# Eight experts on one core: the store of expert 6 goes behind the last load in the GpSimd ring, the store of expert 5 goes out in halves

## The chip, the cores and the metric

The kernel runs on one NeuronCore of a Trainium2 chip. The metric is the device time of one execution in microseconds, as the median of several runs. The profile is that of one execution; its span (first to last instruction) is a little shorter than the time that is measured.

The engines that matter here are PE (matmuls), DVE and ACT (copies out of PSUM, and the ReLU on ACT), GpSimd (POOL in the profile) and SyncE (SP), which here do little but issue DMAs. GpSimd's DMAs form one queue, called the ring below and q0 in the profile; SyncE's form another, q1; ACT has q10. All run on the same 16 DMA engines.

## The reference

Eight experts, each a two-layer perceptron on its own 256 rows, all in float32:

```python
n_experts, capacity, hidden, expert_hidden = 8, 256, 512, 2048
h = np.matmul(x, w1) + b1[:, np.newaxis, :]
h = np.maximum(h, 0)
return (np.matmul(h, w2) + b2[:, np.newaxis, :]).astype(np.float32)
```

One expert has 4 MB of `w1`, 4 MB of `w2`, 0.5 MB of `x` and 0.5 MB of output. No weight is used twice by different experts, so every byte is read once.

## The kernel before

**Staging.** Matmuls are done in fp16. The weights and most of `x` are cast from float32 to fp16 by the DMA that loads them, and all of these loads are issued by GpSimd. `x` of the first two experts comes as float32 by SyncE and ACT, so that the ring can begin with `w1`.

**Per expert.** `first_product(e)` (line 112) makes h transposed, 128 of the 2048 hidden units at a time: four matmuls into one PSUM tile `ph`, then a ReLU with bias on ACT (line 119) into `hT`. In its middle it transposes `x` of the next expert (line 99). `second_product(e)` (lines 162 and 174) starts each of two accumulators `acc` (one for each half `tb` of the rows) with the bias and adds 16 matmuls of 512 columns. The output rows are dealt so that each partition holds two neighbouring rows: its stores are rows of 4 KB per partition.

**Order of the stages.** The loop at the end runs over stages `s`: the first product of expert `s`, then the second product of expert `s - LAG`, with `LAG = 3`. So the second products run three experts behind.

**Order of the DMAs.** The list `ring` is the order, written out by hand, in which GpSimd issues: per stage the loads of `x`, `w1` and `w2`, and from stage 6 on a `flush`, which is the store of an expert done earlier. The list is kept in program order. GpSimd waits at the head of its queue, so what stands behind a waiting issue waits too. By the waits in the trace, a ring transfer also waits for the landing of the eighth one before it.

**The end.** `w2` of the last expert comes in eight pieces, called pieces 1 to 8 below, in this order (rows `j` of the 16, columns):

```python
        (0, 4, 0, H), (4, 7, 0, H), (7, 10, 0, H), (10, 12, 0, H),
        (12, 14, 0, HL), (14, 16, 0, HL), (12, 14, HL, H), (14, 16, HL, H),
```

With `HL = 320`, the last expert's output has a block of 320 columns, which is finished and stored first, and one of 192. `flush(4)` stands between pieces 1 and 2; after piece 8 nothing follows in the ring.

**The stores.** `store(e, ...)` copies the two accumulators to SBUF, one by DVE (line 137), one by ACT (line 138), and then has three ways. The 192-column block of the last expert goes out by SyncE and ACT, one half of the rows each (lines 141 and 142). For `e <= RING` (0 to 4) the store is only noted in `pending`, and `flush` (line 131) issues it from GpSimd at its place in the ring. All others (5, 6 and the 320-column block of 7) are issued by SyncE as soon as the copies are done (line 148); `PARTS` could cut them into groups of partitions, and is empty. The staging tiles of experts 0 to 6 share three buffers; the last expert's have their own.

Of the kernel before, what the change touches and what calls it, by code (L numbers as in the profile page):

```python
# [11 lines left out]
def kernel(  # L12
# [17 lines left out]
    nJ = M // P  # L30
    HL = 320
    LAG = 3
    RING = 4
    PARTS = {}
    nXF32 = 2

    def ordered(ins):
# [95 lines left out]
    def store(e, po, c0, c1, split):  # L133
        w = c1 - c0
        pool = out_pool if w == H else singles
        out_sb = pool.tile([P, nTB, w], fp32, tag=f"out{c0}_{w}", name=f"out{w}")
        nc.vector.tensor_copy(out=out_sb[:, 0, :], in_=po[0])  # L137
        nc.scalar.copy(out=out_sb[:, 1, :], in_=po[1])  # L138
        dst = out[e].rearrange("(p tb) h -> p tb h", tb=nTB)[:, :, c0:c1]
        if split and c1 == H:  # L140
            nc.sync.dma_start(out=dst[:, 0, :], in_=out_sb[:, 0, :])
            nc.scalar.dma_start(out=dst[:, 1, :], in_=out_sb[:, 1, :])
        elif e <= RING:
            pending[e] = (dst, out_sb)
        else:
            step = P // PARTS.get(e, 1)
            for lo in range(0, P, step):
                nc.sync.dma_start(out=dst[lo : lo + step], in_=out_sb[lo : lo + step])

    def second_product(e):  # L150
# [18 lines left out]
        for lo, hi, p0, p1, t in w2_sb[e]:  # L169
            mine = [b for b in blocks if p0 <= b[0] and b[1] <= p1]  # L170
            for tb in range(nTB):
                for j in range(lo, hi):
                    for c0, c1, _, _ in mine:
                        ordered(nc.tensor.matmul(  # L174
                            out=acc[c0, tb],
                            lhsT=hT[e][:, j, tb * P : (tb + 1) * P],
                            rhs=t[:, j - lo, c0 - p0 : c1 - p0],
                            start=False,
                            stop=(j == nJ - 1),
                        ))  # L180
            if hi == nJ:
                for c0, c1, _, _ in mine:
                    store(e, [acc[c0, tb] for tb in range(nTB)], c0, c1, e == E - 1)
# [36 lines left out]
    ring = []  # L220
# [9 lines left out]
    e = E - LAG - 1  # L230
    for piece in (
        (0, 4, 0, H), (4, 7, 0, H), (7, 10, 0, H), (10, 12, 0, H),
        (12, 14, 0, HL), (14, 16, 0, HL), (12, 14, HL, H), (14, 16, HL, H),
    ):
        ring.append((0, load_w2_piece, (E - 1,) + piece))
        if e <= RING:
            ring.append((e + LAG + 1, flush, (e,)))
            e += 1

    for s in range(E + LAG):  # L240
        while ring and ring[0][0] <= s:
# [37 lines left out]
```

## Time and profile before

| | |
|---|---|
| time, median of 3 runs | 185.75 us (185.68 to 185.85) |
| span of the profile | 183.8 us |
| PE busy | 137.3 us, 75% |
| ACT busy | 62.7 us, 34% |
| DVE busy | 13.3 us, 7% |
| GpSimd busy | 21.0 us, 11% |
| mean DMA rate | 221 GB/s (40.58 MB) |
| read from HBM, written to HBM | 71.39 MB, 4.19 MB |
| SyncE store of expert 5 | issued at 160.9, landed 8.2 us later |
| SyncE store of expert 6 | issued at 168.5, landed 7.1 us later |
| ring stores of experts 0 to 4 | landed 48.4, 43.7, 40.1, 28.0 and 18.3 us after issue |
| SyncE store of the 320-column block | issued at 179.5, landed 2.8 us later |

The profile's DMA bytes count a cast load by what it writes, in fp16, while "read from HBM" counts the float32 that it reads; so 1 MB of loads and 1 MB of stores are different amounts of work. The share of DMA engines is the time of their packet records over 16 engines' time, and can go a little over 1 where records overlap. "To landing" is the time from a DMA's issue to its completion; for a ring transfer it includes the wait behind the transfers ahead of it. Times on the engines are those of the trace from the start of the span.

### The profile page before, as it was taken

To read this page: it belongs to the slowest core of one execution; us is meant where nothing else is said; L and a number is where in the kernel's file an instruction comes from. 1 tells how busy PE (TensorE), PEld (TensorE's weight loads), DVE (VectorE), ACT (ScalarE), POOL (GpSimd) and SP (SyncE) were. 2 spreads that over 40 slices of the span, in tenths; PEclk is the share of its full clock that TensorE was granted. 3 is DMA by queue.
4 is the path that set the end of the run, shared out by engine and by line. 5 is a ranking of instruction groups with operands and counts; after the bars stand their busy time and mean duration, and the time that the engine had idled before them with its cause. 6 is when DMAs were issued, how large, how long until landed. Compare 5 with 4: busy or idle time off the path is not lost.

```text
span 183.8 us, 2205 instructions
## 1 busy us (share of the span) xinstructions
PE 137.3 (75%) x946; PEld 98.2 (53%) x946; DVE 13.3 (7%) x22; ACT 62.7 (34%) x138; POOL 21.0 (11%) x44
## 2 busy tenths in 40 slices
PE   0555969487471999569991999529999996998581
PEld 0544959387461846556491846427469543344360
DVE  0320101001000101010100100001010010101000
ACT  0022869578260422715081513605129310101001
POOL 7100030301200011011011002000022004113000
PEclk9999999999876699979999699965999999999998
DMA  5999999899999999999999999899999999999993
GB/s 185 283 207 198 228 228 210 184 233 230 228 203 196 228 228 217 194 216 228 228 210 200 217 228 228 191 266 225 207 200 270 240 209 260 214 275 310 261 151 116
DMA packets 7017, 40.58 MB, mean 221 GB/s; under 512 B 1216, under 2 KB 2256, under 8 KB 4960
## 3 DMA queue, kind: packets, MB, share of 16 engines
q0 software_dynamic: 5584, 37.76, 95.3%
q1 hardware_dynamic: 976, 2.00, 3.1%
q10 hardware_dynamic: 448, 0.69, 1.1%
q8 instruction: 7, 0.11, 0.2%
q14 instruction: 2, 0.02, 0.0%
HBM read 71.39 MB, written 4.19 MB: 411 GB/s over the span
## 4 chain that ended last, share of the span: by engine, by line
DMA 70%; PE 14%; issue 9%; another core or an unknown queue 3%; POOL 2%; ACT 0%; POOLq 0%
DMA x<-in_x_dram 24%; DMA w2sb<-in_w_dram 21%; DMA w1sb<-in_w_dram 13%; DMA w<-in_w_dram 12%; PE ph L112 6%; PE acc L174 6%; PE psx L99 1%; POOL w2sb L84 1%; POOL w1sb L74 1%; POOL out_dram L131 0%; PE acc L162 0%; POOL b_sb L190 0%; POOL ident masks.py:199 0%; POOL ident masks.py:197 0%
## 5 line engine op out<-in xcount | busy, mean ns | idle before, releaser
L112 PE MATMUL ph<-xT,w1sb 128*128 128x256 f16 x512 | 68.2, 299 | 11.6 <-DMA w1sb<-in_w_dram 11.6
L119 ACT ACTIVATE hT<-ph,b1T 128x256 f16<-128x256 f32 x128 | 57.0, 474 | 44.2 <-PE ph L112 44.2
L112 PEld LDWEIGHTS <-w1sb 128*128 128x128 f16 x512 | 61.5, 149 | 17.7 <-DMA w1sb<-in_w_dram 12.6
L174 PE MATMUL acc<-w2sb,hT 128*128 128x512 f16 x224 | 49.5, 379 | 1.6 <-DMA w2sb<-in_w_dram 1.6
L174 PEld LDWEIGHTS <-hT 128*128 128x128 f16 x288 | 27.2, 98 | 35.0 <-issue 9.0
L138 ACT COPY out<-acc 128x512 f32<-128x512 f32 (+2 forms) x9 | 4.9, 543 | 62.0 <-PE acc L174 62.0
L99 PE MATMUL psx<-ident,x 128*128 128x128 f16 x64 | 6.7, 266 | 18.8 <-DMA x<-in_x_dram 18.1
L99 PEld LDWEIGHTS <-x 128*128 128x128 f16 x64 | 5.2, 127 | 19.8 <-DMA x<-in_x_dram 19.0
L105 DVE COPY xT<-psx 128x1024 f16<-128x1024 f16 x8 | 5.5, 692 | 82.2 <-PE psx L99 82.2
L74 POOL DMA_DIRECT2D w1sb<-in_w_dram x8 | 4.4, 554 | 59.6 <-PE ph L112 58.8
L137 DVE COPY out<-acc 128x512 f32<-128x512 f32 (+2 forms) x9 | 5.7, 632 | 75.5 <-PE acc L174 75.5
L174 PE MATMUL acc<-w,hT 128*128 128x320 f16 (+1 forms) x64 | 7.7, 272 | 3.8 <-DMA w<-in_w_dram 3.7
L84 POOL DMA_DIRECT2D w2sb<-in_w_dram x8 | 4.3, 537 | 49.4 <-PE acc L174 49.4
L205 PE MATMUL pb<-ident,b_rows 16*64 16x16 f32 x64 | 3.7, 265 | 6.8 <-DMA b_rows<-in_b_dram 6.8
L205 PEld LDWEIGHTS pb<-ident,b_rows 16*64 16x64 f32 x64 | 3.6, 198 | 6.8 <-issue 6.8
L90 POOL DMA_DIRECT2D w<-in_w_dram x8 | 5.0, 623 | 13.0 <-DMA w2sb<-in_w_dram 8.8
L119 ACT ACT_TABLE_LOAD x1 | 1.3, 1283 | 11.2 <-DVE b1T L213 11.2
L131 POOL DMA_DIRECT2D out_dram<-out x5 | 2.7, 540 | 19.5 <-ACT out L138 13.1
L162 PE MATMUL acc<-b_sb,ones 1*128 1x512 f16 (+2 forms) x18 | 4.8, 355 | 0.0
L68 POOL DMA_DIRECT2D x<-in_x_dram x6 | 3.3, 546 | 7.2 <-DMA w2sb<-in_w_dram 5.1
L162 PEld LDWEIGHTS <-ones 1*128 1x128 f16 x18 | 1.1, 92 | 2.2 <-issue 2.1
L200 DVE CAST x<-x 128x1024 f16<-128x1024 f32 x2 | 1.4, 694 | 4.5 <-DMA x<-in_x_dram 4.5
(9 smaller groups left out, 2.6 us busy)
## 6 DMA issues: line engine op xcount, KB each, us to landing
w1sb<-in_w_dram POOLq DMA_DIRECT2D x8, 2048.0 KB, 33.7
w2sb<-in_w_dram POOLq DMA_DIRECT2D x6, 2048.0 KB, 45.7
out_dram<-out POOLq DMA_DIRECT2D x5, 512.0 KB, 40.1
w2sb<-in_w_dram POOLq DMA_DIRECT2D x2, 1024.0 KB, 24.6
x<-in_x_dram POOLq DMA_DIRECT2D x6, 256.0 KB, 39.0
out_dram<-out SPq DMA_DIRECT2D x2, 512.0 KB, 7.6
w<-in_w_dram POOLq DMA_DIRECT2D x2, 384.0 KB, 20.8
x<-in_x_dram SPq DMA_DIRECT2D x1, 512.0 KB, 4.7
```

The lines of the kernel that those rows point to most:

```text
L74: ordered(nc.gpsimd.dma_start(out=w1_sb[e], in_=w1[e].rearrange("(p kc) m -> p kc m", kc=nKC)))
L84: ordered(nc.gpsimd.dma_start(out=t[:, lo : lo + step, :], in_=src[:, lo : lo + step, :]))
L90: ordered(nc.gpsimd.dma_start(out=t, in_=src[:, lo:hi, c0:c1]))
L99: ordered(nc.tensor.transpose(out=pt[:, kc, tb * P : (tb + 1) * P], in_=x16[e][:, tb, :].rearrange("p (q kc) -> p q kc", kc=nKC)[:, :, kc] ...
L105: nc.vector.tensor_copy(out=xT[e], in_=pt)
L112: ordered(nc.tensor.matmul(out=ph, lhsT=w1_sb[e][:, kc, :].rearrange("p (q j) -> p q j", j=nJ)[:, :, j], rhs=xT[e][:, kc, :], start=(kc == 0),
L119: nc.scalar.activation(out=hT[e][:, j, :], in_=ph, func=mybir.ActivationFunctionType.Relu, bias=b1T[:, j, e : e + 1], scale=1.0,)
L137: nc.vector.tensor_copy(out=out_sb[:, 0, :], in_=po[0])
L138: nc.scalar.copy(out=out_sb[:, 1, :], in_=po[1])
L162: ordered(nc.tensor.matmul(out=t, lhsT=ones1, rhs=b2_sb[0:1, e * H + c0 : e * H + c1], start=True, stop=False,))
L174: ordered(nc.tensor.matmul(out=acc[c0, tb], lhsT=hT[e][:, j, tb * P : (tb + 1) * P], rhs=t[:, j - lo, c0 - p0 : c1 - p0], start=False, sto ...
L205: ordered(nc.tensor.matmul(out=pb[s * 64 : (s + 1) * 64, j, :, :], lhsT=b1_rows.rearrange("r (q j) -> r q j", j=nJ)[:, :, j], rhs=ident[0 ...
```

## The change

The store of expert 6 (512 KB) is no longer issued by SyncE when its copies are done, but noted and issued by GpSimd behind piece 8, as the last entry of the ring. It is meant to keep the store out of the way of the last pieces of the weights. The store of expert 5, still on SyncE, is issued as two DMAs of 64 partitions (256 KB) each. The stores of experts 0 to 4 and those of the last expert keep their places.

```diff
-    RING = 4
-    PARTS = {}
+    LATE = (6,)
+    RING = (0, 1, 2, 3, 4) + LATE
+    PARTS = {5: 2}
...
-        elif e <= RING:
+        elif e in RING:
             pending[e] = (dst, out_sb)
         else:
             step = P // PARTS.get(e, 1)
...
         ring.append((0, load_w2_piece, (E - 1,) + piece))
-        if e <= RING:
+        if e in RING and e not in LATE:
             ring.append((e + LAG + 1, flush, (e,)))
             e += 1
+    for e in LATE:
+        ring.append((e + LAG + 1, flush, (e,)))
```

## The prediction

> **What bounds the kernel now.** I read the page first, then the chain of waits, then the last 25 us by timeline, windows and DMA queues.
>
> The page shows which resource never rests: the row of DMA shares, the two queues, and the chain by engine.
>
> ```profile
> DMA  5999999899999999999999999899999999999993
> ...
> q0 software_dynamic: 5584, 37.76, 95.3%
> q1 hardware_dynamic: 976, 2.00, 3.1%
> ...
> DMA 70%; PE 14%; issue 9%; another core or an unknown queue 3%; POOL 2%; ACT 0%; POOLq 0%
> ```
>
> The 16 DMA engines are at 0.9 or more from the second slice to the last but one, and the GpSimd ring (q0) alone fills 95.3% of them. PE is busy 75% and waits. So what counts is when the last bytes of the weights land, and what else the engines carry before that.
>
> The chain of waits (start, length, what) shows how the end comes about:
>
> ```profile
> 113.67 39.47 DMA w2sb<-in_w_dram
> 153.14 0.28 issue
> 153.43 21.99 DMA w<-in_w_dram
> 175.41 0.04 issue
> 175.45 3.88 PE acc L174 x32
> 179.34 0.02 issue
> 179.35 0.50 PE acc L174 x4
> 179.85 0.02 issue
> 179.88 0.32 ACT out L138
> ```
>
> The last expert's w2 comes in eight pieces. The chain runs through the third, issued at 153.43 and landed at 175.41; then PE does the rest of the product in 4.40 us. By the view of line 90, window by window, the later pieces land at 176.6 (154.68 + 21.9), 177.5 (159.48 + 18.0), 178.2 (164.41 + 13.8), 178.8 (166.13 + 12.7) and 179.34 (169.34 + 10.0). The last weight load, at 179.35, follows the landing of piece 8 at once, so PE and the DMA tail are tied. In the timeline PE has only two short idle stretches after 175.45:
>
> ```profile
> 178.30 0.89 PEld L174 LDWEIGHTS <-hT 128*128 128x128 f16 x8 [0.16 <-issue]
> ...
> 179.35 0.26 PEld L174 LDWEIGHTS <-hT 128*128 128x128 f16 x3 [0.17 <-issue]
> ```
>
> Without these PE needs 4.40 - 0.33 = 4.1 us after piece 3. If all pieces come earlier by the same time, the end moves by that time.
>
> Now the store in question. By the view of line 148, expert 6's SyncE store is issued at 168.5 and lands 7.1 us later, at 175.6, about when piece 3 lands. The DMA view of 172 to 176 shows what it takes (packets, MB, share of 16 engines):
>
> ```profile
> q0 software_dynamic: 409, 0.55, 76.9%
> q1 hardware_dynamic: 141, 0.51, 33.8%
> ```
>
> In those 4 us the ring moved 0.55 MB and SyncE's queue 0.51 MB: the whole of the store. The windows compare the stretches (after the clock: DMA share, GB/s):
>
> ```profile
> 156.00:160.00 4.00, 4.00 (x20) 1.73 (x18) 0.69 (x1) 0.00 (x0) 0.52 (x1) 1.00 1.03 215
> ...
> 172.00:176.00 4.00, 2.02 (x17) 1.55 (x17) 0.00 (x0) 0.00 (x0) 0.00 (x0) 1.00 1.11 266
> 176.00:178.00 2.00, 2.00 (x20) 1.64 (x18) 0.00 (x0) 0.00 (x0) 0.00 (x0) 1.00 1.29 172
> 178.00:180.00 2.00, 1.82 (x15) 1.09 (x13) 0.78 (x2) 0.55 (x2) 0.00 (x0) 1.00 0.27 32
> ```
>
> PE is idle for half of 172 to 176, waiting for pieces, while the engines carry the store; from 178 to 180 they are nearly empty (0.27).
>
> **What the Trainium skill says.** Three places on its page "DMA: Bandwidth & Descriptors" bear on this. Section "Queues, rings and completion order": each engine takes turns between the queues that have work, packet by packet, and within a ring descriptors are consumed in order. The trace agrees with the first: the store takes 33.8% beside the ring's 76.9%. So a store on SyncE's queue overtakes loads issued long before it, and one behind the last load in the ring does not. Section "Issuing engines are not separate DMA queues": all issuers run on the same 16 engines, so the change saves no bandwidth; it can only alter the order. The trace agrees, the shares adding up to 1.03 to 1.11. Section "Rules for kernel authors": of two transfers to disjoint partition halves it says "Don't bother — they serialize". No row of the kernel before shows halves.
>
> **The change part by part.**
>
> *Store 6 leaves SyncE's queue.* Its cost in engine time is 33.8% of 4 us = 1.35 us. Two other readings bound it. From the page, q1 took 3.1% of 183.8 = 5.7 us for 2.00 MB, so 0.524 MB cost 1.49 us. From the rates, the ring made 0.55 MB in 4 us = 138 GB/s; without the store it makes 215 with large packets (156 to 160) and 172 with the smallest (176 to 178). Taking 195, between them, it lost 57 x 4 = 0.23 MB, or 1.17 us; with 215 it lost 0.31 MB, or 1.43 us. Records overlap somewhat, the share being 1.11 in this stretch and not 1; the highest share that I can blame on the pieces alone is between 1.03 and 1.29. I take 1.35 / 1.09 = 1.24 us, and keep 0.9 and 1.5 as ends. So piece 3 lands at 175.4 - 1.2 = 174.2, piece 8 at 179.34 - 1.24 = 178.1. PE: from piece 3, 174.2 + 4.1 = 178.3; from piece 8, 178.1 + 0.5 = 178.6. The later sets it: 178.6, against 179.85.
>
> *Store 6 joins the GpSimd ring behind piece 8.* One issue of 0.54 us (the row of line 131), on an engine that has nothing behind it. It waits for three things: the issue of piece 8, ending at 170.05 (169.34 + 0.71); the ACT copy of expert 6, ending at 168.47; and, if the pattern of the waits on GpSimd holds (each ring transfer waits for the eighth before it: piece 3 for w2 of expert 5, piece 4 for the store of expert 2), the landing of store 4, at 152.0 + 18.3 = 170.3. So it is issued by about 171, seven us before its turn. Nobody waits for its landing but the end of the program. Its bytes flow as the engines run out of pieces: before, the DMA share began to fall at 177.8 and was nothing at 179.1 to 179.4; 1.24 earlier and 1.35 longer, the store is through by 179.5. That lies beside PE's last matmuls, the copies and the issue of the last stores.
>
> *The last stores.* The 320-column store was issued at 179.49 and landed 2.8 us later; it is now issued at 178.25. Its own bytes come late in those 2.8 us: the engines stood empty from 179.4 and the packet records of that queue begin at about 181.2, 1.7 us after the issue. So they begin at 179.9, 0.4 us after store 6 is through. I charge nothing; if the two meet, the bound is 0.5 us of shared engines. The stretch from the end of PE to the end of the span, 183.8 - 179.85 = 3.95 us, is kept.
>
> *Store 5 in two halves.* One more SyncE issue of 0.35 us, with nothing behind it on SyncE until 178, and the same bytes at the same place in the stream, so zero; bounds -0.2 and +0.3 us, since no row shows 64-partition stores. It had 8.2 us to landing before, and nobody waits for its buffer: it goes into the third of the three, and the only later tile of that pool, expert 6's, takes the first.
>
> *The queue tests (line 143 and the loop that fills the ring)* move nothing else: stores 0 to 4 stay between the same loads.
>
> Sum: 185.75 - 1.24 = 184.5 us, a span near 182.6.
>
> **The rivals.** *Partial gain.* The slowest engine is the one that counts, and it may gain less than the mean, or the last stores meet store 6 and give 0.5 us back. For it: the fall of the share from 177.8 to 179.1 shows that engines do not end together. Against it: a store of 128 equal rows loads all engines alike. Gain 0.4 to 0.9, some 0.65: 185.1.
>
> *No change.* The store used time that the loads could not, or the tail eats the gain whole. For it: the share of 1.11 against 1.03, and 266 GB/s moved against 215. Against it: a loaded byte is counted as fp16 but read as fp32, so bytes of loads and stores are not alike, and the ring's own rate fell to 138. 185.7.
>
> *Slower.* The last stores are treated as store 6 was: amid the ring's traffic a SyncE store took 7.1 to 8.2 us to land, after it 2.8. If the ring still holds store 6 when the 320-column store is issued, it may lose part of the difference of 4.3; with half of it, 2.15, the time is 185.75 - 1.24 + 2.15 = 186.7. Against it: only 1.3 us of the ring is left at that moment, not a stream of many us.
>
> **How the numbers follow.** Full gain (0.9 to 1.5) 0.62 at 184.5; partial 0.18 at 185.1; none 0.11 at 185.7; slower 0.09 at 186.7. A gain of over 0.2% is one of over 0.37 us, so faster 0.80, same 0.11, slower 0.09. The low end is the upper bound of the store's cost with the halves' best, 185.75 - 1.5 - 0.2 = 184.05, rounded down to 183.9 for the small difference between runs; the high end, 185.6, takes in the partial gain and leaves out most of the last two cases.
>
> **What would show it.** Right: in 172 to 176 the hardware queue carries next to nothing; piece 3 lands near 174.2 and piece 8 near 178.1; the chain still goes through a piece and PE; the ring is busy until about 179.5; the last stores still land 2.4 to 2.8 us after issue. Wrong: piece 3 landing where it did (the store was free), the last stores taking 4 us or more (the slower rival), or store 5's halves landing much later than 8.2 us after issue with pieces 1 to 3 later too.

## The result and the profile after

| | before | after |
|---|---|---|
| time, median of 6 runs each | 185.72 us | 184.31 us |
| ratio, 95% interval | | 0.9926 (0.9913 to 0.9939) |
| span of the profile | 183.8 us | 182.4 us |
| piece 1 lands | 169.06 | 169.09 |
| piece 3 lands | 175.41 | 174.00 |
| piece 8 lands | 179.31 | 178.02 |
| store 6 lands | 175.58 | 179.27 |
| end of the last matmul | 179.85 | 178.56 |
| last of the last stores lands | 182.88 | 181.52 |

The change makes the kernel 1.41 us faster (0.74%, interval 0.61 to 0.87%). The table's last seven rows are from the two traces. Up to piece 2 the landings of the pieces agree within 0.1 us; from piece 3 on the pieces, PE's end and the last stores are all 1.3 to 1.4 us earlier. Store 6 alone lands later.

The page of the kernel after, the same rows as were shown of before (slices of the DMA share; queues with packets, MB and share; chain by engine):

```profile
DMA  5999999999899989999999999999999999999994
...
q0 software_dynamic: 5728, 38.28, 96.7%
q1 hardware_dynamic: 848, 1.47, 2.3%
...
DMA 82%; PE 12%; POOL 2%; issue 1%; ACT 0%; POOLq 0%
```

The total of both queues is 39.8 MB, as before: 0.52 MB moved from q1 to q0 and nothing was saved. The DMA engines remain the bound, at 82% of the chain. Its end (start, length, what):

```profile
169.38 8.64 DMA w<-in_w_dram
178.02 0.04 issue
178.06 0.50 PE acc L175 x4
178.56 0.02 issue
178.59 0.32 ACT out L139
```

Before, the chain went through piece 3 and 36 matmuls; now it goes through piece 8 and its own four matmuls. Both were nearly tied before; the tie has tipped to the landing, as the prediction's working had it. The timeline of after shows how PE lives between pieces 2, 3, 6 and 8 (start, length, instruction, count, idle time before it and what ended it):

```profile
172.19 1.47 PE L175 MATMUL acc<-w,hT 128*128 128x320 f16 x12 [1.15 <-DMA w<-in_w_dram]
...
174.04 4.51 PE L175 MATMUL acc<-w,hT 128*128 128x320 f16 x36 [0.38 <-DMA w<-in_w_dram]
...
176.95 0.89 PEld L175 LDWEIGHTS <-hT 128*128 128x128 f16 x8 [0.22 <-issue]
...
178.06 0.26 PEld L175 LDWEIGHTS <-hT 128*128 128x128 f16 x3 [0.23 <-issue]
```

The wait for piece 3 shrank from 1.74 us to 0.38 us. That is where PE's time came from, but only because piece 8 came earlier too: in ring_before_8 below, the wait for piece 3 is as short (0.34 us), piece 8 lands as late as before, and PE ends at 179.90, no earlier than before. The two small gaps behind it grew from 0.33 to 0.45 us in all; each ends 0.04 to 0.05 us after a landing, of piece 6 (176.90) and of piece 8 (178.02), so PE waits there for pieces too.

The DMA view of after for 172 to 176, the four us in which SyncE's queue had carried 0.51 MB:

```profile
q0 software_dynamic: 878, 0.79, 121.5%
q14 instruction: 1, 0.01, 0.5%
```

SyncE's queue is absent, and the ring moves 0.79 MB of loads instead of 0.55. The share over 1 (records of small packets overlap) says that the share is a poor measure here; the bytes are not. The windows of after (after the clock: DMA share, GB/s) show where the store went:

```profile
172.00:176.00 4.00, 3.43 (x30) 2.71 (x30) 0.00 (x0) 0.00 (x0) 0.00 (x0) 1.00 1.22 200
176.00:178.00 2.00, 1.96 (x16) 1.31 (x15) 0.49 (x1) 0.32 (x1) 0.00 (x0) 1.00 1.17 279
178.00:180.00 2.00, 0.49 (x4) 0.26 (x3) 0.36 (x1) 0.43 (x2) 0.00 (x0) 1.00 0.47 176
```

PE is busy 3.43 of the first 4 us instead of 2.02. From 176 to 178 the engines move 279 GB/s instead of 172. By the packet records the store's 4 KB packets begin at 176.1, beside those of the last pieces, and the last of them ends at 178.9, beside PE's last matmuls and the copies; the store lands at 179.27.

### The profile page after: what moved, and what is told of

Its sections match the earlier page's. It is cut to its first block, busy times and chain, and to the rows that moved or that the text cites. A ratio compares the mean times of both kernels' runs of the same rounds, so it can differ in the third digit from the quotient of the medians.

```text
span 182.4 us, 2206 instructions
## 1 busy us (share of the span) xinstructions
PE 138.0 (76%) x946; PEld 98.3 (54%) x946; DVE 13.3 (7%) x22; ACT 62.8 (34%) x138; POOL 21.6 (12%) x45
## 4 chain that ended last, share of the span: by engine, by line
DMA 82%; PE 12%; POOL 2%; issue 1%; ACT 0%; POOLq 0%
DMA x<-in_x_dram 24%; DMA w2sb<-in_w_dram 24%; DMA w<-in_w_dram 21%; DMA w1sb<-in_w_dram 13%; PE ph L113 7%; PE acc L175 4%; PE psx L100 1%; POOL w2sb L85 1%; POOL w1sb L75 1%; PE acc L163 0%; POOL out_dram L132 0%; POOL b_sb L191 0%; POOL ident masks.py:199 0%; POOL ident masks.py:197 0%; ACT out L139 0%
## 5 line engine op out<-in xcount | busy, mean ns | idle before, releaser
L113 PE MATMUL ph<-xT,w1sb 128*128 128x256 f16 x512 | 69.2, 302 | 10.0 <-DMA w1sb<-in_w_dram 10.0
L100 PE MATMUL psx<-ident,x 128*128 128x128 f16 x64 | 6.2, 254 | 19.9 <-DMA x<-in_x_dram 19.2
L132 POOL DMA_DIRECT2D out_dram<-out x6 | 3.3, 542 | 20.7 <-ACT out L139 13.1
```

The lines of the kernel that those rows point to most:

```text
L100: ordered(nc.tensor.transpose(out=pt[:, kc, tb * P : (tb + 1) * P], in_=x16[e][:, tb, :].rearrange("p (q kc) -> p q kc", kc=nKC)[:, :, kc] ...
L113: ordered(nc.tensor.matmul(out=ph, lhsT=w1_sb[e][:, kc, :].rearrange("p (q j) -> p q j", j=nJ)[:, :, j], rhs=xT[e][:, kc, :], start=(kc == 0),
```

## The experiments

The theory: the store cost its engine time because its bytes went ahead of the last pieces; behind them there is idle DMA time that holds it. The rivals: the halves of store 5 bring part; the queue matters and not the place; the tail gives part of the gain back. Ratios are to runs of the kernel before on the same chip (median 185.66 to 185.75 us).

| run | time, us | ratio, 95% interval |
|---|---|---|
| late_only | 184.45 | 0.9929 (0.9917 to 0.9941) |
| halves_only | 186.15 | 1.0024 (1.0015 to 1.0033) |
| ring_before_8 | 184.97 | 0.9965 (0.9952 to 0.9978) |
| no_store_6 | 184.55 | 0.9933 (0.9922 to 0.9945) |
| late_quarters | 184.85 | 0.9955 (0.9943 to 0.9968) |
| sync_behind_320 | 186.23 | 1.0027 (1.0018 to 1.0035) |
| late_5_and_6 | 183.43 | 0.9879 (0.9866 to 0.9893) |
| late_4_5_6 | 183.53 | 0.9882 (0.9868 to 0.9895) |
| nine_dmas | 186.13 | 1.0023 (1.0013 to 1.0033) |
| after_again (the changed kernel) | 184.50 | 0.9934 (0.9920 to 0.9948) |

**Store 6 late, store 5 whole** (late_only), from the changed kernel:

```diff
-    PARTS = {5: 2}
+    PARTS = {}
```

> Store 6 behind piece 8 as in the changed kernel, store 5 whole as before. Theory (the place of store 6 is all): 184.35 us, within 0.2 us of the changed kernel's 184.31; piece 8 lands near 178.0. Rival (the halves bring part of the 1.41 us, the prediction having given store 6 only 1.24): 184.5 to 184.8, and the other part in the run with the halves alone.

Measured 184.45 us, and 0.9929 against 0.9926 and 0.9934 for the changed kernel: the same. From piece 1 to piece 8 it takes 8.92 us, in the changed kernel 8.93, in the kernel before 10.25. The whole gain is that of the late store.

**Store 5 in halves alone** (halves_only), from the kernel before:

```diff
-    PARTS = {}
+    PARTS = {5: 2}
```

> Store 5 in two halves, store 6 by SyncE at once as before. Theory: no change, 185.7 us, within 0.2 us of the kernel before. Rival (the halves help): 185.2 to 185.5; piece 1 or 2 would then land earlier than 169.0 and 172.2.

Both theories missed: it is slower, by 0.45 us (0.24%). The stream is not to blame. Pieces 3 and 8 land at 175.53 and 179.46, both 0.1 to 0.15 later, and so does the last store (182.99 against 182.88). But from that landing to the end of the span there are 1.36 us instead of 0.93. The waits of SyncE show it; first the kernel before, then this run (engine and line, what it waited for: us in total, times, longest):

```profile
SPq L274 <- DMA out_dram<-out: 1.6, 3, 1.2
```

```profile
SPq L274 <- DMA out_dram<-out: 2.1, 1, 2.1
```

At the end of the program SyncE waits for the DMA semaphores (the counters that tell that a DMA has landed), two in each wait. In the kernel before, the late landings were waited for by the last waits of that row, and those ahead were already behind it. In this run SyncE stands 2.1 us in the second wait of the row, and goes through the seven waits behind it, some 0.06 us each, after the last landing: 0.43 us in all. SyncE and ACT issue nine DMAs here instead of eight. In the trace these DMAs have eight semaphores, one each in the kernel before; with nine, SyncE's 192-column store, the last to land, has that of a load from the start of the program once more, and this one stands in the second wait of the row.

**Nine DMAs without halves** (nine_dmas) tests that reading: the load of `b1` at the start of the kernel before is cut in two, store 5 stays whole.

```diff
-    nc.scalar.dma_start(out=b1_rows, in_=b1.rearrange("e (s i) -> (e s) i", s=2))
+    b1_src = b1.rearrange("e (s i) -> (e s) i", s=2)
+    for lo in (0, E):
+        nc.scalar.dma_start(out=b1_rows[lo : lo + E], in_=b1_src[lo : lo + E])
```

> The kernel before, with the load of b1 on ACT cut into two of 8 rows: nine DMAs from SyncE and ACT, as in the run with the halves alone, but store 5 whole. Theory (the ninth moves the last landing ahead of SyncE's other end waits): the last landing near 182.9, the stretch after it 1.3 to 1.4 us instead of 0.93, SyncE waiting for a landing once instead of three times; 186.1 to 186.2 us. Rival (the halves of store 5 cost it by themselves): 185.7 us and 0.93.

186.13 us; the last landing at 182.92, and 1.35 us from there to the end. The waits of SyncE in this run:

```profile
SPq L276 <- DMA out_dram<-out: 2.3, 1, 2.3
```

Again one wait instead of three, and again the last store to land has that early semaphore. So the 0.45 us belong to the ninth DMA, in both places where it was tried, and not to the halves. Store 6 was issued 1.2 us later in this run, piece 3 landed 1.0 us earlier (174.41) and piece 8 only 0.14; PE ended 0.14 us earlier, so an early piece 3 alone is again worth nothing.

**Store 5 in quarters beside the late store** (late_quarters), `PARTS = {5: 4}` in the changed kernel:

> As the changed kernel, but store 5 in four DMAs of 32 partitions. Theory: splitting costs nothing where the bytes flow, pieces and last stores land as in the changed kernel; but SyncE and ACT then issue ten DMAs instead of eight. In the run with the halves alone (nine instead of eight) the last landing moved only 0.11 us, while the stretch from there to the end of the span grew from 0.93 to 1.36 us, SyncE's waits on the DMA semaphores at the end standing behind the last one to land instead of ahead of it. So 184.6 to 184.8 us, with about 1.3 us after the last landing. Rival (halves slow the stream itself): pieces 1 to 3 land later than 169.1, 172.2 and 174.0, and the stretch after the last landing stays 0.93. Third: nothing, 184.3.

184.85 us, with 1.29 us after the last landing, which SyncE waits for in the third wait of the row, with six behind it; from piece 2 to piece 8 it takes 5.83 us, in the changed kernel 5.87. The changed kernel has eight such DMAs, since it takes store 6 away and adds a half of store 5, and late_only has seven: both have 0.92 to 0.93 us at the end.

**The place or the queue** (ring_before_8): store 6 in the ring ahead of piece 8, store 5 whole, from the changed kernel:

```diff
-    for piece in (
+    for n, piece in enumerate((
...
-    ):
+    )):
+        if n == 7:
+            ring.append((6 + LAG + 1, flush, (6,)))
...
-    for e in LATE:
-        ring.append((e + LAG + 1, flush, (e,)))
```

> Store 6 in the GpSimd ring, but ahead of piece 8 instead of behind it; store 5 whole. Theory (what counts is which loads the store's bytes precede, not which queue carries them): pieces 3 to 7 land 1.2 to 1.3 us earlier as in the changed kernel, piece 8 lands at about 179.3 as in the kernel before, and the time is 185.4 to 185.8 us. Rival (what counts is that the store leaves SyncE's queue, whose packets take turns with the ring's): 184.3 to 184.6 us.

The pieces do as the theory says: 3 to 7 land at 174.17 to 177.62, 1.2 us earlier than before, and piece 8 at 179.37, as before. The time is 184.97 us, below what I expected of the theory and above the rival's, so both missed. The timeline of the run shows why:

```profile
174.21 3.99 PE L175 MATMUL acc<-w,hT 128*128 128x320 f16 x32 [0.34 <-DMA w<-in_w_dram]
...
178.36 0.61 SPq L149 DMA_DIRECT2D out_dram<-out  x1
179.41 0.49 PE L175 MATMUL acc<-w,hT 128*128 128x192 f16 x4 [1.21 <-DMA w<-in_w_dram]
...
180.16 0.34 SPq L142 DMA_DIRECT2D out_dram<-out  x1
180.29 0.37 ACTq L143 DMA_DIRECT2D out_dram<-out  x1
```

PE waits 1.21 us for piece 8, as expected, but the 320-column store is issued at 178.36, 1.13 us earlier than before, since its block needs pieces 1 to 6 alone. By the time of the 192-column stores its bytes are nearly out of the way: these land 1.74 and 1.94 us after issue instead of 2.72 and 2.37. So the tail after PE holds a queue of its own, which my expectation had left out. PE ends where it did before, and what is gained is gained behind it. The place matters within the same ring: one entry further ahead, the store costs about half of the gain (the six runs spread over 0.9 us, so the half is rough).

**Without the store** (no_store_6): `flush` drops expert 6's entry; store 5 whole.

```diff
         dst, src = pending.pop(e)
+        if e in LATE:
+            return
```

> The store of expert 6 is left out altogether (its rows of the output are never written); store 5 whole. Theory (behind piece 8 the store lies wholly beside the end of the work): the same time as the changed kernel, 184.2 to 184.35 us. Rival (the tail gives part of the gain back, the last stores waiting for store 6): 183.6 to 184.0 us, with the last stores landing sooner after their issue than the 2.3 to 2.8 us of the changed kernel.

184.55 us, 0.9933: no faster than with the store (184.45 in late_only), and its last stores land 2.83, 2.73 and 2.38 us after issue. The store behind piece 8 costs nothing that can be measured.

**Late, but by SyncE** (sync_behind_320), from the kernel before, with both SyncE stores kept in program order:

```diff
-        elif e <= RING:
+        elif e <= RING or e == 6:
             pending[e] = (dst, out_sb)
...
+            if e == E - 1:
+                d6, s6 = pending.pop(6)
+                ordered(nc.sync.dma_start(out=d6, in_=s6))
```

> Store 6 stays on SyncE but is issued behind the 320-column store of the last expert, ahead of the 192-column one; store 5 whole. Theory (which loads and stores its bytes precede is what counts): the pieces land as in the changed kernel, 174.0 and 178.0, but the last store now lands 1.0 to 1.4 us later after the end of PE: 185.3 to 185.7 us. Rival (leaving the loads alone is enough, wherever the store ends up): 184.3 us.

The pieces land as in the changed kernel (3 at 174.14, 8 at 178.11), with the store on the queue that it had before: for the loads it is the place that counts and not the queue. But the time is 186.23 us, slower than before: the last store lands at 183.58. It is issued 0.80 us later than in the changed kernel, behind one more issue on SyncE, and its bytes stand behind store 6's. Leaving the loads alone is not enough; the store must not precede the last stores either. I had expected 0.5 to 0.9 us less, from a delay of 1.0 to 1.4 us behind PE's end; it was 2.0. Store 6 landed 1.85 us behind the 320-column store (181.09 and 182.94). That no run has store 6 in the ring ahead of piece 3, where the queue alone would have changed, stays a gap.

**Two late stores** (late_5_and_6), and **three** (late_4_5_6), all stores whole:

```diff
-    LATE = (6,)
+    LATE = (5, 6)
-    PARTS = {5: 2}
+    PARTS = {}
```

> Stores 5 and 6 both behind piece 8 in the ring. If the tail still has room: pieces another 1.25 us earlier, piece 3 at 172.8, piece 8 at 176.8, the ring's stores through at 179.3 as now, beside which the last stores take turns: 183.3 to 183.8 us. If the last stores are held up by the ring's 2.6 us of queued stores as stores 5 and 6 were amid the stream (7 to 8 us to landing): they land 4 to 5 us after issue instead of 2.3 to 2.8, and the time is 184.3 to 185.5 us.

> Stores 4, 5 and 6 all behind piece 8. The pieces come 2.5 us earlier than in the changed kernel only if PE can follow: it ends expert 6 at 167.7 and needs some 7.5 us for the last expert, so not before 175.3 to 175.8; the engines must still carry all bytes, so the ring ends at 179.3 as now and the last stores lie among its bytes: 183.3 to 184.0 us, no better than with two late stores. If the last stores are held up: 185 us or more.

Two late stores beat both kernels: 183.43 us, 2.3 us less than before. Pieces 3 and 8 land at 172.74 and 176.69, each 1.3 us earlier than in the changed kernel. Part of that comes back: the last stores now land 3.18, 3.01 and 2.73 us after issue. Three bring nothing more, 183.53 us: piece 8 lands at 175.69, but the last stores take 4.46, 4.33 and 3.99 us. The windows of the two runs, first with two late stores, then with three:

```profile
176.00:178.00 2.00, 1.22 (x12) 0.79 (x9) 0.85 (x2) 0.74 (x2) 0.00 (x0) 1.00 0.90 341
178.00:180.00 2.00, 0.00 (x0) 0.00 (x0) 0.00 (x0) 0.00 (x0) 0.00 (x0) 1.00 0.87 317
```

```profile
176.00:178.00 2.00, 0.22 (x3) 0.00 (x0) 0.36 (x1) 0.32 (x1) 0.00 (x0) 1.00 1.02 411
178.00:180.00 2.00, 0.00 (x0) 0.00 (x0) 0.00 (x0) 0.00 (x0) 0.00 (x0) 0.97 0.76 278
```

In the changed kernel the engines had a share of 0.47 from 178 to 180; with two late stores it is 0.87, and the idle time is used up. With three, PE is done by 176.2 and the program waits for bytes alone. In the profiled run with two late stores PE had a granted clock of 0.72 from 153 to 159, and from 153 on its chain goes through PE alone; with three the clock was 1.00 there. How much of the difference of 1.0 us between the two ends of PE (177.22 and 176.22) is the clock's, the runs don't show.

## Why the prediction was right

**The bound and the mechanism held.** The store's bytes stood ahead of pieces 3 to 8 and cost them their engine time; late_only and no_store_6 show that this is the whole of the gain, sync_behind_320 and ring_before_8 that it is the place: on its old queue but behind the loads the store leaves the pieces alone, and in the ring ahead of piece 8 it holds that piece back.

**The size of the store's cost** was taken a little small. I had 1.35 us of engine time and divided it by 1.09 for overlapping records, 1.24 us. Piece 3 came 1.41 us earlier and piece 8 1.29, so the 1.35 themselves would have been the better value. The 1.09 was a choice between shares of 1.03 and 1.29 and not measured; records overlap without the store as well (share 1.22 from 172 to 176 after the change), so dividing may have taken off something that was not the store's. The estimate from the rates, 1.17 to 1.43 us, held as well.

**PE after piece 3**: 4.1 us from there gave 178.3, piece 8 gave 178.6 and was to set the end; it did, at 178.56.

**The place behind piece 8**: I had it issued by about 171 and through by 179.5; it was issued at 171.34, a us after the landing of store 4, and landed at 179.27. **The last stores** were to be undisturbed, the 320-column one issued at 178.25; it was issued at 178.14, and the three landed 2.75, 2.71 and 2.30 us after issue, before 2.83, 2.72 and 2.37. One reading in the prediction was off: the packets of the 320-column store begin before the change at 180.75, 1.26 us after the issue, and not at 181.2. After the change they begin at 179.38, 0.45 us behind the last packet of store 6, so the margin of 0.4 us came out all the same, since store 6 was through earlier than I had it.

**The halves at zero** was right for this change but not for the reason given. The bytes do cost nothing, but a further DMA on SyncE or ACT can cost 0.45 us at the end of the program (halves_only, nine_dmas), more than the 0.3 I had as a bound. Here it was not paid because the change takes one such DMA away and adds one; I had not thought of that, and the zero was luck.

**The slower rival** did not come about here; with a longer queue a part of it does. What the ring still holds when the 320-column store is issued, from that issue to the landing of the ring's last store, was 1.1 us in the changed kernel, 2.3 with two late stores and 3.7 with three; the three last stores then took 0, at most 0.4 and 1.6 us longer to land than in the kernel before. The first packet of the 320-column store came 1.24, 1.26 and 1.62 us after its issue, so these stores shared the engines with the ring more than they waited for a start, as stores 5 and 6 had (last section). The **partial gain** did not happen: pieces 3 to 8 all came forward by 1.3 to 1.4 us, and the last stores did not meet store 6. The trace does not tell the 16 engines apart, so whether a single engine gained less can be judged by the landings alone.

## What to carry to other kernels

Where the DMA engines are the bound up to the last load, try to queue a store that is ready before that load behind it, as long as the engines have idle time between the last load and the last store. The amount that fits is what they can move in that stretch: here a second store of 512 KB still brought 0.9 us, and a third nothing. What helped here was the place and not the queue; ask which loads and which last stores a store's bytes precede. Look also at the stretch between the last landing and the end of the span: one more DMA from SyncE or ACT, even at the start of the program, lengthened it by 0.4 us where the last landing came to be waited for early in SyncE's row.

## What the runs showed of the hardware that was not expected

- The stretch after the last landing was 0.92 to 0.99 us with seven or eight DMAs from SyncE and ACT, 1.35 and 1.36 with nine and 1.29 with ten. In these runs it follows from where in SyncE's row of end waits the last landing is waited for. With six it was 1.04, though the last landing is waited for at the end of the row; where that 0.1 us comes from is open.
- 512 KB behind the 320-column store on SyncE's queue, with the ring empty, landed 1.85 us after it, while the ring's late stores followed each other at 1.24 to 1.27 us (413 to 423 GB/s). That is not the speed of the queue: by the packet records store 6 begins at 180.8, beside the last packets of ACT's store, and ends at 182.4, and from 181 to 182 SyncE's queue moved 385 GB/s.
- A SyncE store issued while the ring had many us of loads ahead had its first packet 3.4 to 3.9 us after the issue (by the packet records of the kernel before, 160.94 to 164.52 for store 5 and 168.49 to 171.94 for store 6), against 1.2 to 1.3 us where the ring held little or nothing (179.49 to 180.75 for the 320-column store). With two late stores, 2.3 us of the ring, it was still 1.26 us, with three, 3.7 us of the ring, 1.62 us. What the delay hangs on wasn't tried.
